# Experts' first product: both activation halves in one 512-column matmul, and every other weight subtraction on GpSimd

## The chip, the cores and the metric

The kernel runs on one core of one Trainium2 chip. The metric is device time in microseconds, the median of the timed runs. A core has five engines with an instruction queue each: PE (TensorE, matmuls, with the weight loads shown as PEld), DVE (VectorE), ACT (ScalarE), POOL (GpSimd) and SP (SyncE, which here issues the loads). Matmuls read their operands from SBUF and write to PSUM, in banks of 512 fp32 numbers per partition.

## The reference

Two transformer blocks run one after the other on 256 tokens of width 1024. The change concerns the feed-forward part of the first one, a layer of 16384 single-neuron experts:

```
q = (t @ w_peer_q) ...                       # two half queries for each of 8 heads
s1, s2 = scores of q against 128 + 128 sub-keys
v1, i1 = top_k(s1, 16); v2, i2 = top_k(s2, 16)
sc, pos = top_k(all 256 sums v1 + v2, 16)    # 16 experts for each head
gates = softmax(sc)
act = gelu(einsum('nkd,nd->nk', expert_u[e], xt), approximate=False)
return einsum('nk,nkd->nd', g * act, expert_v[e])
```

The kernel does not gather the chosen experts. It computes Gelu of the product of all 16384 rows of `expert_u` with all tokens (the first product), builds a dense matrix of gates G that is zero for experts not chosen, and multiplies the weighted activations with all of `expert_v` (the second product).

## The kernel before

Numbers are fp32, but each matrix operand is split into two numbers of a shorter format (fp32r): a high half, which is the operand rounded by a cast, and a low half, which is the operand minus the high half. A product is then the sum of three matmuls: high by high, high weights by low activations, and low weights by high activations (`mm3`, lines 226 to 228).

A unit of weights is 128 rows by 1024. `load` brings one with one DMA from SP, and `halve` splits it: a cast on ACT writes the high half (line 209), a subtraction on DVE writes the low half (line 211).

The first product takes 128 blocks of 128 experts. `up()` does one block: it issues the split of the next block's weights, keeps three loads ahead, runs `mm3` into one PSUM bank (24 matmuls of 256 columns, eight groups of three), and Gelu on ACT from PSUM into a staging tile (line 818). Every second block the tile is stored to DRAM by a DMA from ACT. The second product later reads it back.

Work of the router is woven between the blocks by `beside()`: each generator yields a cost in ns, and as many blocks are issued as that cost divided by a slack. `route` picks the top experts on DVE (slack 1300 ns, DVE's order kept as written); its last part, `keys`, compares, multiplies and reduces pieces of 256 and 512 elements (lines 676 to 680). `gates` then builds G (slack 2050 ns): for each group of eight tokens DVE makes one-hot tiles in fp16 by four instructions of 1024 elements (lines 729 to 736), PE multiplies them in 16 matmuls that `flush()` places behind a block's own (lines 744 and 745), and ACT moves the result to G (line 746). Except for DVE during `route`, the order on an engine is that of a scheduler.

Weight halves live in pools of two buffers each. While `route` runs there is a second pair of pools (`room(qs, 2)`), so four high and four low buffers; in the gates and after them there are two of each. PSUM banks for products come from `bank()`, which turns among two banks plus those that `more_banks` adds: four while `route` runs, two afterwards.

Of the kernel before, what the change touches and what calls it, by code (L numbers as in the profile page):

```python
# [8 lines left out]
F32 = mybir.dt.float32  # L9
# [10 lines left out]
T = 256  # L20
# [116 lines left out]
class Net:  # L137
# [65 lines left out]

    def halve(self, raw):
        nc = self.nc
        whi, wlo = self.turns[0]
        self.turns = self.turns[1:] + self.turns[:1]
        hi = whi.tile([128, 1024], F32R, name="hi_t", tag="hi")
        nc.scalar.copy(hi, raw)  # L209
        lo = wlo.tile([128, 1024], F32R, name="lo_t", tag="lo")  # L210
        nc.vector.tensor_tensor(lo, raw, hi[:].bitcast(F32), op=OP.subtract)  # L211
        return hi, lo
# [17 lines left out]
    def proj(self, src, x, n, s=slice(0, None), ps=None):  # L230
        ps = self.bank() if ps is None else ps
        self.mm3(ps[:, :n], self.early.pop(0) if self.early else self.unit(src), x[0], x[1], s)
        return ps[:, :n]

    def act_table(self, name):
# [526 lines left out]
    def experts(self, h, follow):  # L762
# [4 lines left out]
        with ExitStack() as es:  # L767
# [7 lines left out]
            self.slots = [pool.tile([128, T], F16, name=f"slot{i}") for i in range(4)]  # L775
            xh = pool.tile([128, KC, T], F32R, name="yh")
            xl = pool.tile([128, KC, T], F32R, name="yl")
            x = (xh, xl)
            qs = ExitStack()
            self.room(qs, 2)  # L780
            self.more_banks(qs, 2)
            qp = qs.enter_context(tc.tile_pool(name="pq", bufs=1))
# [25 lines left out]
            def up():  # L808

                nonlocal a, b, w  # L810
                nxt = self.halve(raw.pop(0)) if b + 1 < NB else None
                ahead(3)
                ps = self.bank()
                self.mm3(ps[:, :T], w, xh, xl)
                flush()
                if b % NG == 0:
                    a = stage.tile([128, NG, T], F32, name="ge_t", tag="ge")
                nc.scalar.activation(a[:, b % NG, :], ps[:, :T], AF.Gelu)
                if b % NG == NG - 1:
                    nc.scalar.dma_start(act[b // NG], a)  # L820
                w = nxt
                b += 1

            def flush():
# [29 lines left out]
            while b < NB:  # L854
                up()
            xs.close()
            self.manual = ExitStack()
# [374 lines left out]


class Acc:

# [75 lines left out]
```

## Time and profile before

| | us |
|---|---|
| median of 3 timed runs | 1465.78 (1465.11 to 1466.89) |
| the profiled execution | 1465.32, span of its instructions 1463.5 |
| first product: routing | about 192 to 405 |
| first product: gates, then a tail | about 405 to 580 |
| second product | about 580 to 960 |
| busy: PE / DVE / ACT / POOL | 1445.6 / 1089.7 / 744.6 / 0.2 |

The time of an engine is its busy time, from records whose matmul ends are modelled: a matmul record includes its latency, so the distance from one start to the next says what it costs. An idle time before an instruction is shown with the instruction that ended it. Rows of DVE and ACT that overlap by a few per cent are instructions whose record starts before that of the one ahead ends.

### The profile page before, as it was taken

What the parts mean: (1) busy time and instruction counts of PE and PEld (TensorE: products, weight loads), DVE (VectorE), ACT (ScalarE), POOL (GpSimd) and SP (SyncE); (2) the same over time, 40 slices, a digit from 0 to 9 for tenths busy, and PEclk for the clock granted to TensorE, in tenths of its full rate; (3) what the DMA queues carried; (4) which work ended last, traced back from release to release, by engine and by line L of the source; (5) the groups of instructions that cost most, each with busy time, mean ns of one, the idle gap of its engine ahead of it and who ended that gap; (6) DMA issues with size and microseconds to landing.
All of it is one profiled execution on the core that took longest, in us unless ns stands there. A gap on an engine that the chain in (4) does not pass through costs nothing.

```text
span 1463.5 us, 29428 instructions
## 1 busy us (share of the span) xinstructions
PE 1445.6 (99%) x12086; PEld 1415.1 (97%) x12086; DVE 1089.7 (74%) x1819; ACT 744.6 (51%) x1157; POOL 0.2 (0%) x4
## 2 busy tenths in 40 slices
PE   7999999999999999999999999999999999999998
PEld 7998999999999999999999999999988999999997
DVE  6975889989889997677777777797766656765554
ACT  6556554445456665544444444454455444744444
POOL 0000000000000000000000000000000000000000
PEclk9999999999999999999999999999999999999999
DMA  7333456767755556777777777745533655566662
GB/s 276 116 109 104 151 187 218 238 226 229 229 170 185 187 188 203 251 245 229 230 230 227 230 228 230 220 150 171 162 127 116 181 184 184 188 208 185 186 186 72
DMA packets 86646, 279.32 MB, mean 191 GB/s; under 512 B 9760, under 2 KB 10480, under 8 KB 86384
## 3 DMA queue, kind: packets, MB, share of 16 engines
q1 hardware_dynamic: 77296, 260.67, 56.9%
q10 hardware_dynamic: 9216, 16.78, 3.0%
q8 instruction: 94, 1.54, 0.4%
q14 instruction: 40, 0.33, 0.1%
HBM read 259.52 MB, written 17.83 MB: 189 GB/s over the span
## 4 chain that ended last, share of the span: by engine, by line
PE 94%; DVE 3%; ACT 2%; DMA 1%; issue 1%; SPq 0%; DVEq 0%; ACTq 0%
PE mm_t L226 18%; PE mm_t L228 18%; PE mm_t L227 18%; PE acc L265 10%; PE acc L266 10%; PE acc L264 10%; PE ga_t L744 1%; PE ga_t L745 1%; ACT hi_t L209 1%; DVE lo_t L211 1%; PE g_t L483 1%; DMA raw_t<-in_w 0%; PE sc_t L624 0%; PE lg_t L950 0%; PE oo_t L976 0%
## 5 line engine op out<-in xcount | busy, mean ns | idle before, releaser
L211 DVE TENSOR_TENSOR lo_t<-raw_t,hi_t 128x1024 fp32r<-128x1024 f32 x456 | 554.7, 1221 | 209.3 <-ACT hi_t L209 207.4
L209 ACT CAST hi_t<-raw_t 128x1024 fp32r<-128x1024 f32 x456 | 476.2, 1048 | 454.5 <-PE mm_t L227 312.1
L226 PE MATMUL mm_t<-yh,hi_t 128*128 128x256 f32 x1024 | 293.0, 286 | 0.0
L265 PE MATMUL acc<-vl_t,hi_t 128*128 128x256 f32 x1024 | 290.2, 283 | 0.5 <-DVE vl_t L219 0.4
L228 PE MATMUL mm_t<-yh,lo_t 128*128 128x256 f32 x1024 | 290.3, 284 | 0.1
L264 PE MATMUL acc<-vh_t,hi_t 128*128 128x256 f32 x1024 | 290.0, 283 | 0.0
L266 PE MATMUL acc<-vh_t,lo_t 128*128 128x256 f32 x1024 | 290.0, 283 | 0.0
L227 PE MATMUL mm_t<-yl,hi_t 128*128 128x256 f32 x1024 | 289.9, 283 | 0.0
L265 PEld LDWEIGHTS acc<-vl_t,hi_t 128*128 128x128 f32 x1024 | 196.7, 192 | 0.9 <-DVE vl_t L219 0.9
L228 PEld LDWEIGHTS mm_t<-yh,lo_t 128*128 128x128 f32 x1024 | 196.4, 192 | 1.1 <-DVE lo_t L211 0.8
L227 PEld LDWEIGHTS mm_t<-yl,hi_t 128*128 128x128 f32 x1024 | 196.6, 192 | 0.1
L264 PEld LDWEIGHTS acc<-vh_t,hi_t 128*128 128x128 f32 x1024 | 196.7, 192 | 0.0
L226 PEld LDWEIGHTS mm_t<-yh,hi_t 128*128 128x128 f32 x1024 | 196.4, 192 | 0.2
L266 PEld LDWEIGHTS acc<-vh_t,lo_t 128*128 128x128 f32 x1024 | 196.7, 192 | 0.0
L226 PE MATMUL mm_t<-ah,hi_t 128*128 128x256 f32 (+2 forms) x448 | 130.0, 290 | 0.0
L228 PE MATMUL mm_t<-ah,lo_t 128*128 128x256 f32 (+2 forms) x448 | 127.3, 284 | 0.0
L227 PE MATMUL mm_t<-al,hi_t 128*128 128x256 f32 (+2 forms) x448 | 126.9, 283 | 0.0
L226 PE MATMUL mm_t<-u,hi_t 128*128 128x256 f32 (+1 forms) x384 | 112.2, 294 | 7.7 <-ACT hi_t L209 7.3
L218 ACT CAST vh_t<-va_t 128x512 fp32r<-128x512 f32 x64 | 39.7, 620 | 149.2 <-DVE va_t L872 144.1
L228 PE MATMUL mm_t<-u,lo_t 128*128 128x272 f32 (+1 forms) x384 | 111.5, 291 | 0.5 <-DVE lo_t L211 0.5
L227 PE MATMUL mm_t<-u,hi_t 128*128 128x256 f32 (+1 forms) x384 | 110.6, 289 | 0.0
L227 PE MATMUL mm_t<-ol,hi_t 128*128 128x256 f32 x384 | 108.0, 281 | 0.3 <-DVE ol L219 0.3
(383 smaller groups left out, 2633.7 us busy)
## 6 DMA issues: line engine op xcount, KB each, us to landing
raw_t<-in_eu SPq DMA_DIRECT2D x128, 512.0 KB, 3.9
raw_t<-in_ev SPq DMA_DIRECT2D x128, 512.0 KB, 4.3
raw_t<-in_w2c SPq DMA_DIRECT2D x40, 512.0 KB, 3.6
act<-ge_t ACTq DMA_DIRECT2D x64, 256.0 KB, 3.3
va_t<-act SPq DMA_DIRECT2D x64, 256.0 KB, 3.3
raw_t<-in_w SPq DMA_DIRECT2D x25, 512.0 KB, 3.9
raw_t<-in_w2qkv SPq DMA_DIRECT2D x24, 512.0 KB, 3.6
raw_t<-in_wg SPq DMA_DIRECT2D x22, 512.0 KB, 4.2
```

The lines of the kernel that those rows point to most:

```text
L209: nc.scalar.copy(hi, raw)
L211: nc.vector.tensor_tensor(lo, raw, hi[:].bitcast(F32), op=OP.subtract)
L218: self.nc.scalar.copy(hi, x)
L226: nc.tensor.matmul(ps, hi[:, ks], xhi[:, k, s], start=k == 0, stop=False)
L227: nc.tensor.matmul(ps, hi[:, ks], xlo[:, k, s], start=False, stop=False)
L228: nc.tensor.matmul(ps, lo[:, ks], xhi[:, k, s], start=False, stop=k == KC - 1)
L264: mm(out, hi, a[0], start=first and opens, stop=False, skip_group_check=True)
L265: mm(out, hi, a[1], start=False, stop=False, skip_group_check=True)
L266: mm(out, lo, a[0], start=False, stop=last, skip_group_check=True)
L483: nc.tensor.matmul(ps[:, 2 * c + w, :].rearrange("p (n j) -> p n j", j=m), k, half(k, 1)[:, 0], start=c + w == 0, stop=True, skip_group_ch ...
L744: nc.tensor.matmul(out, o2[:, u, :], oh[:, :, u, :], start=i == 0, stop=False, skip_group_check=True)
L745: nc.tensor.matmul(out, o2[:, u, :], ol[:, :, u, :], start=False, stop=True, skip_group_check=True)
```

## The change

Three things change, all in the first product.

The activation halves lie in one tile `yy`, high and low half of the same 128 rows side by side. `pairs()` takes the place of `mm3`: the high weights stream both halves in one matmul of 512 columns that fills a whole bank (the first 256 columns hold high by high, the others high by low), and the low weights add their 256 columns to the first half. The last of the eight groups has the two in reverse order. A block is 16 matmuls.

The two halves of the bank are added afterwards, by `finish()`, which `up()` calls once the next block's matmuls are issued: ACT copies the second half to the staging tile, DVE adds the first half to it, and ACT applies Gelu in place. One bank more stays after `route` (three in place of two), and one fewer of the extra ones ends with it, so four remain while it runs.

The low half of every other block's weights is subtracted on POOL in place of DVE (64 of 128).

```diff
--- before.py
+++ after.py
@@ -201,14 +201,14 @@
         self.nc.sync.dma_start(raw, src)
         return raw
 
-    def halve(self, raw):
+    def halve(self, raw, vector=True):
         nc = self.nc
         whi, wlo = self.turns[0]
         self.turns = self.turns[1:] + self.turns[:1]
         hi = whi.tile([128, 1024], F32R, name="hi_t", tag="hi")
         nc.scalar.copy(hi, raw)
         lo = wlo.tile([128, 1024], F32R, name="lo_t", tag="lo")
-        nc.vector.tensor_tensor(lo, raw, hi[:].bitcast(F32), op=OP.subtract)
+        (nc.vector if vector else nc.gpsimd).tensor_tensor(lo, raw, hi[:].bitcast(F32), op=OP.subtract)
         return hi, lo
 
     def unit(self, src):
@@ -231,6 +231,19 @@
         ps = self.bank() if ps is None else ps
         self.mm3(ps[:, :n], self.early.pop(0) if self.early else self.unit(src), x[0], x[1], s)
         return ps[:, :n]
+
+    def pairs(self, w, x, s=slice(0, T)):
+
+
+        ps = self.bank()
+        pair = ps[:].rearrange("p (n t) -> p n t", n=2)
+        hi, lo = w
+        for k in range(KC):
+            ks = slice(k * 128, (k + 1) * 128)
+            parts = [(pair, hi[:, ks], x.both[:, k, :, s]), (ps[:, 0:T], lo[:, ks], x.both[:, k, 0, s])]
+            for out, a, y in parts if k < KC - 1 else reversed(parts):
+                self.nc.tensor.matmul(out, a, y, start=k == 0 and out is pair, stop=k == KC - 1 and out is pair, skip_group_check=True)
+        return ps
 
     def act_table(self, name):
         self.tc.keep_in_program_order(self.nc.scalar.preload_act_table_set(name))
@@ -773,12 +786,12 @@
             psp = xs.enter_context(tc.tile_pool(name="pep", bufs=2, space=PSUM))
             self.iota = pool.tile([128, 128], F16, name="iota16")
             self.slots = [pool.tile([128, T], F16, name=f"slot{i}") for i in range(4)]
-            xh = pool.tile([128, KC, T], F32R, name="yh")
-            xl = pool.tile([128, KC, T], F32R, name="yl")
-            x = (xh, xl)
+            x = Halves(pool, T, "yy")
+            xh, xl = x
             qs = ExitStack()
             self.room(qs, 2)
-            self.more_banks(qs, 2)
+            self.more_banks(xs)
+            self.more_banks(qs)
             qp = qs.enter_context(tc.tile_pool(name="pq", bufs=1))
             with tc.tile_pool(name="pen", bufs=2) as npool:
                 self.load_con(npool, "conp")
@@ -807,19 +820,31 @@
 
             def up():
 
-                nonlocal a, b, w
-                nxt = self.halve(raw.pop(0)) if b + 1 < NB else None
+                nonlocal b, w
+                nxt = self.halve(raw.pop(0), b % 2 == 1) if b + 1 < NB else None
                 ahead(3)
-                ps = self.bank()
-                self.mm3(ps[:, :T], w, xh, xl)
+                ps = self.pairs(w, x)
                 flush()
-                if b % NG == 0:
-                    a = stage.tile([128, NG, T], F32, name="ge_t", tag="ge")
-                nc.scalar.activation(a[:, b % NG, :], ps[:, :T], AF.Gelu)
-                if b % NG == NG - 1:
-                    nc.scalar.dma_start(act[b // NG], a)
+                finish()
+                ready.append((ps, b))
                 w = nxt
                 b += 1
+
+            ready = []
+
+            def finish():
+
+                nonlocal a
+                for ps, b in ready:
+                    if b % NG == 0:
+                        a = stage.tile([128, NG, T], F32, name="ge_t", tag="ge")
+                    y = a[:, b % NG, :]
+                    nc.scalar.copy(y, ps[:, T:2 * T])
+                    nc.vector.tensor_tensor(y, ps[:, 0:T], y, op=OP.add)
+                    nc.scalar.activation(y, y, AF.Gelu)
+                    if b % NG == NG - 1:
+                        nc.scalar.dma_start(act[b // NG], a)
+                ready.clear()
 
             def flush():
                 for f in self.after:
@@ -853,6 +878,7 @@
             vp0 = gside.enter_context(tc.tile_pool(name="vp0", bufs=1, side="right"))
             while b < NB:
                 up()
+            finish()
             xs.close()
             self.manual = ExitStack()
             self.manual.enter_context(tc.manual_schedule(engines=ordered))
@@ -1231,6 +1257,21 @@
                     nc.sync.dma_start(self.out[:, f:f + n, :], y)
 
 
+class Halves:
+
+
+    def __init__(self, pool, n, name):
+        self.both = pool.tile([128, KC, 2, n], F32R, name=name)
+
+    def __getitem__(self, i):
+        if not 0 <= i < 2:
+            raise IndexError(i)
+        return self.both[:, :, i, :]
+
+    def __len__(self):
+        return 2
+
+
 class Acc:
```

On PE, in routing, two blocks meet like this before (each row is one matmul: output, moving operand, weights; numbers tell buffers apart):

```order
L227 MATMUL mm_t_2478<-yl_1923,hi_t_2427 128x256
L228 MATMUL mm_t_2478<-yh_1922,lo_t_2429 128x256
L226 MATMUL mm_t_2478<-yh_1922,hi_t_2427 128x256
L227 MATMUL mm_t_2478<-yl_1923,hi_t_2427 128x256
L228 MATMUL mm_t_2478<-yh_1922,lo_t_2429 128x256
L226 MATMUL mm_t_2523<-yh_1922,hi_t_2472 128x256
L227 MATMUL mm_t_2523<-yl_1923,hi_t_2472 128x256
L228 MATMUL mm_t_2523<-yh_1922,lo_t_2474 128x256
```

And now:

```order
L245 MATMUL mm_t_2413<-yy_1922,hi_t_2380 128x512
L245 MATMUL mm_t_2413<-yy_1922,lo_t_2382 128x256 x2
L245 MATMUL mm_t_2413<-yy_1922,hi_t_2380 128x512
L245 MATMUL mm_t_2452<-yy_1922,hi_t_2407 128x512
L245 MATMUL mm_t_2452<-yy_1922,lo_t_2409 128x256
L245 MATMUL mm_t_2452<-yy_1922,hi_t_2407 128x512
```

A group of three has become a pair, the next block's low weights are wanted by its second matmul, and the high weights of a block are held until its last one.

On DVE, in the gates, before (`o_t`, `ol_t` and `oh_t` are the one-hot tiles, `lo_t` the low half of weights):

```order
L211 TENSOR_TENSOR lo_t<-raw_t,hi_t 128x1024
L729 TENSOR_TENSOR o_t<-iota_1917,slot_1919 128x1024
L732 TENSOR_TENSOR ol_t<-ioT,run_5713 128x1024
L735 TENSOR_TENSOR oh_t<-ol_t,run_5750 128x1024
L211 TENSOR_TENSOR lo_t<-raw_t,hi_t 128x1024
L736 TENSOR_TENSOR ol_t<-ol_t,run_5753 128x1024
L211 TENSOR_TENSOR lo_t<-raw_t,hi_t 128x1024
```

And now, where `ge_t<-mm_t,ge_t` is the add:

```order
L211 TENSOR_TENSOR lo_t<-raw_t,hi_t 128x1024
L843 TENSOR_TENSOR ge_t<-mm_t,ge_t 128x256
L742 TENSOR_TENSOR o_t<-iota_1917,slot_1919 128x1024
L745 TENSOR_TENSOR ol_t<-ioT,run_5630 128x1024
L843 TENSOR_TENSOR ge_t<-mm_t,ge_t 128x256
L748 TENSOR_TENSOR oh_t<-ol_t,run_5661 128x1024
L749 TENSOR_TENSOR ol_t<-ol_t,run_5664 128x1024
L742 TENSOR_TENSOR o_t<-iota_1917,slot_1919 128x1024
L745 TENSOR_TENSOR ol_t<-ioT,run_5630 128x1024
L211 TENSOR_TENSOR lo_t<-raw_t,hi_t 128x1024
```

Every block has an add in DVE's row, with gate work and a subtraction behind it, and every second subtraction has left the row for POOL, where the 64 stand alone.

On ACT, in the gates, the evacuation of a block before (`G` is the move of a gate group out of PSUM):

```order
L209 CAST hi_t_6988<-raw_t_6833 128x1024
L746 ACTIVATE G_5227<-ga_t_6960 128x512
L746 ACTIVATE G_5227<-ga_t_6970 128x512
L818 ACTIVATE ge_t_6924<-mm_t_6935 128x256
L820 DMA act53_1897<-ge_t_6924 128x512
L209 CAST hi_t_7032<-raw_t_6877 128x1024
```

And now, for two blocks:

```order
L842 COPY ge_t_6610<-mm_t_6523 128x256
L209 CAST hi_t_6620<-raw_t_6483 128x1024
L759 ACTIVATE G_4775<-ga_t_6590 128x512
L759 ACTIVATE G_4775<-ga_t_6600 128x512
L844 ACTIVATE ge_t_6610<-ge_t_6610 128x256
L842 COPY ge_t_6610<-mm_t_6573 128x256
L844 ACTIVATE ge_t_6610<-ge_t_6610 128x256
L846 DMA act56_1900<-ge_t_6610 128x512
L209 CAST hi_t_6658<-raw_t_6521 128x1024
```

The second block's copy stands behind a cast, two moves of G and the first block's Gelu, and its own Gelu, which waits for DVE's add, stands ahead of the next cast.

Outside the first product the order on every engine is the same as before.

## Rows read from the trace of the kernel before

**Rows 1.** Page, part 1: engine, busy us (share of the span), instructions.
```profile
PE 1445.6 (99%) x12086; PEld 1415.1 (97%) x12086; DVE 1089.7 (74%) x1819; ACT 744.6 (51%) x1157; POOL 0.2 (0%) x4
```

**Rows 2.** Windows by stage: length, busy us (count) of PE, PEld, DVE, ACT, POOL; clock.
```profile
192.00:405.00 213.00, 213.00 (x1776) 213.00 (x1777) 193.76 (x548) 103.03 (x153) 0.00 (x0) 1.00 0.70 227
424.50:567.00 142.50, 142.50 (x1415) 141.34 (x1414) 131.88 (x152) 89.20 (x175) 0.00 (x0) 1.00 0.59 186
567.00:580.00 13.00, 13.00 (x127) 12.91 (x126) 7.44 (x8) 6.86 (x13) 0.00 (x0) 1.00 0.70 221
```

**Rows 3.** Page, part 5: group, count | busy us, mean ns | idle before it.
```profile
L211 DVE TENSOR_TENSOR lo_t<-raw_t,hi_t 128x1024 fp32r<-128x1024 f32 x456 | 554.7, 1221 | 209.3 <-ACT hi_t L209 207.4
L209 ACT CAST hi_t<-raw_t 128x1024 fp32r<-128x1024 f32 x456 | 476.2, 1048 | 454.5 <-PE mm_t L227 312.1
L226 PE MATMUL mm_t<-yh,hi_t 128*128 128x256 f32 x1024 | 293.0, 286 | 0.0
```

**Rows 4.** Timeline, routing, PE: start us, us, what.
```profile
260.01 0.28 PE L226 MATMUL mm_t<-yh,hi_t 128*128 128x256 f32 x1
260.37 0.28 PE L226 MATMUL mm_t<-yh,hi_t 128*128 128x256 f32 x1
```

**Rows 5.** Windows, two periods of the gates (columns as in rows 2).
```profile
430.23:440.78 10.55, 10.55 (x106) 10.46 (x105) 10.37 (x14) 6.62 (x14) 0.00 (x0) 1.00 0.63 198
440.78:451.33 10.55, 10.55 (x106) 10.46 (x105) 9.65 (x12) 6.55 (x14) 0.00 (x0) 1.00 0.61 189
```

**Rows 6.** Timeline, gates, DVE.
```profile
503.73 1.22 DVE L211 TENSOR_TENSOR lo_t<-raw_t,hi_t 128x1024 fp32r<-128x1024 f32 x1
504.86 1.22 DVE L729 TENSOR_TENSOR o_t<-iota,slot 128x1024 f16<-128x1024 f16 x1
506.00 0.68 DVE L732 TENSOR_TENSOR ol_t<-ioT,run 128x1024 f16<-128x1024 f16 x1
506.71 0.69 DVE L735 TENSOR_TENSOR oh_t<-ol_t,run 128x1024 f16<-128x1024 f16 x1
507.32 1.22 DVE L211 TENSOR_TENSOR lo_t<-raw_t,hi_t 128x1024 fp32r<-128x1024 f32 x1
```

**Rows 7.** Timeline, gates, ACT.
```profile
502.14 1.05 ACT L209 CAST hi_t<-raw_t 128x1024 fp32r<-128x1024 f32 x1 [1.35 <-PE mm_t L227]
503.10 1.08 ACT L746 ACTIVATE G<-ga_t 128x512 f32<-128x512 f32 x2
505.98 1.05 ACT L209 CAST hi_t<-raw_t 128x1024 fp32r<-128x1024 f32 x1 [1.53 <-PE mm_t L227]
```

**Rows 8.** Waits in the gates: us in total, times, longest us.
```profile
ACT hi_t L209 <- PE mm_t L227: 51.4, 40, 1.6
```

**Rows 9.** Groups by form, gates: the comparison, once a gate group.
```profile
L729 DVE TENSOR_TENSOR o_t<-iota,slot 128x1024 f16<-128x1024 f16 x32 | 39.0, 1218 | 0.0
```

**Rows 10.** Timeline, mixer, PE: 416 columns and what follows.
```profile
63.67 0.35 PE L395 MATMUL z_t<-sp,negtri_r 128*128 128x416 f32 x1
63.85 0.29 PE L395 MATMUL z_t<-sp,negones_r 128*128 128x144 f32 x2
64.33 0.35 PE L395 MATMUL z_t<-sp,negtri_r 128*128 128x416 f32 x1
64.52 0.29 PE L395 MATMUL z_t<-sp,negones_r 128*128 128x144 f32 x2
```

**Rows 11.** Groups by form: one PSUM input on ACT and on DVE.
```profile
L818 ACT ACTIVATE ge_t<-mm_t 128x256 f32<-128x256 f32 x128 | 48.5, 379 | 3.5 <-PE mm_t L228 3.5
L1195 DVE TENSOR_TENSOR sg_t<-sg_t,mm_t 128x256 f32<-128x256 f32 x20 | 8.4, 420 | 12.1 <-PE mm_t L228 12.1
```

**Rows 12.** Groups by form: key steps of routing, DVE.
```profile
L680 DVE TENSOR_REDUCE ki<-eq 128x32 f32<-128x512 f16 x16 | 18.1, 1128 | 0.5
L678 DVE TENSOR_TENSOR eq<-eq,kf 128x256 f16<-128x256 f16 x32 | 12.1, 421 | 0.0
L676 DVE TENSOR_TENSOR eq<-io,df 128x256 f16<-128x256 f16 x32 | 7.8, 287 | 0.0
```

## The prediction

> **What bounds the kernel now.** Read the page's first part first: the reader is to see TensorE (PE) at 99% of the span and GpSimd (POOL) idle but for 0.2 us [rows 1]. Then the windows, since that share is an average: the change touches only the stage of the first product, which falls into routing (192 to 405 us), gates (424.5 to 567) and a short tail [rows 2]. In all three the TensorE clock is 1.00, its 2.4 GHz level, and PE is busy without a gap. VectorE (DVE) is the next engine: 193.8 of 213 us in routing, 131.9 of 142.5 in the gates.
>
> Then the costliest groups [rows 3]: one line of the product has 1024 matmuls, and three lines of that form make 128 blocks of 24. The 286 ns of one are latency, not price. The price is the distance of starts: three matmuls take 260.37 - 260.01 = 0.36 us, so 120 ns each and 2.88 us a block [rows 4]. Its 256 columns at 2.4 GHz are 107 ns, so 13 ns come on top.
>
> In the gates three blocks and two gate groups repeat every 10.55 us [rows 5]. Three blocks are 8.64 us, so the matmuls of a gate group cost (10.55 - 8.64) / 2 = 0.95 us. DVE works 10.37 and 9.65 us of two such periods. Its instructions there nearly all read two tensors from SBUF, and they start 1.13 us apart behind a 1.22 us subtraction or comparison and about 0.7 us behind the shorter ones [rows 6]. The cast of a high half waits for TensorE: 51.4 us in 40 waits, since there are only two high buffers there [rows 8], and it runs when a block ends (502.14, 505.98) [rows 7]. There are 32 gate groups, so 16 such periods [rows 9].
>
> **The change, part by part.**
>
> *Matmuls.* 24 of 256 columns become 8 of 512 and 8 of 256. Columns stay the same; 8 starts and 8 weight loads go. The trace has no such matmul of 512 columns. The floor by the clock is 512 / 2.4 = 213 ns; the ceiling, two of today's, is 240. The nearest row is the one of 416 columns, which is followed after 0.18 and 0.19 us [rows 10]; with 96 more columns at 120 / 256 ns, that is 225 to 235. I take 230, with 120 for the other one: 350 ns a pair in place of 360, 80 ns a block, 2.80 us a block. For all 128 blocks this is 10 us at most, unless the second one of a pair also gets cheaper: 213 + 107 = 320 would be 41 us.
>
> *Evacuation.* Before, one Gelu reads PSUM (379 ns). Now ScalarE (ACT) copies half of the bank, DVE adds the other half, and ACT runs Gelu from SBUF. I price copy and Gelu at that row's 0.38 us each, and the add at the 0.42 us of an add or product of one PSUM and one SBUF tensor of the same size [rows 11]. ACT has room (103 of 213 us in routing) [rows 2]. DVE gains 0.42 us a block and loses 1.13 / 2. What is new is the coupling: the add waits for the copy, the copy for the block's end, and behind the add stands all of DVE's routing or gate work and the next subtraction.
>
> *Half the subtractions on POOL.* No row shows a POOL instruction of this kind. From below it costs what DVE takes, 1.22 us; from above, two blocks, 5.6 us, at which POOL alone would set the pace. I take 2.44, twice the DVE row. The Trainium skill (GPSIMD Engine Reference, Performance versus the Vector engine) gives 4497 ns for 2048 elements of such an add, so by estimate 2.25 for 1024; with it the sum below would be 4.6 us lower. Whether it also stops DVE no row shows either: beside each other it costs DVE nothing, in turn it costs the whole 2.44 us. I choose in turn, the dearer end: nearly all of DVE's work in the gates has the same form as POOL's, two inputs from SBUF, and that is the stage with the least spare time. The Trainium skill (SBUF — State Buffer, Who interferes with whom) says the same: a VectorE instruction with two SBUF inputs and a GpSimd one that reads SBUF exclude each other for a whole instruction. By that rule the gates get slower, without it they stay as they are; no run here shows it yet.
>
> *Routing, 74 blocks.* TensorE saves 74 x 0.08 = 5.9 us. High buffers are four deep there, so a late POOL result is covered. DVE's work stays in its written order. In the key steps, 16 pieces of 1.13 + 2 x 0.42 + 2 x 0.29 = 2.55 us [rows 12] stand against a budget of 1700 / 1300 = 1.31 blocks: per block 2.55 / 1.31 + 0.61 + 0.42 = 2.98 us, above the 2.80 of TensorE. Before, DVE could run ahead to make that good; now the adds tie it to TensorE. 0.18 x 1.31 x 16 = 3.7 us back.
>
> *Gates, 16 periods of three blocks.* TensorE would need 10.55 - 0.24 = 10.31 us. DVE's two-input work is 2 x (1.13 + 0.7 + 0.7 + 0.7) = 6.46, plus 1.5 subtractions of 1.13 = 1.7, together 8.2; POOL's in turn 1.5 x 2.44 = 3.66. That is 11.8 us if the adds (3 x 0.42) all fall beside POOL, and 1.2 us more than before. 16 x 1.2 = 19.4 us. The order of ACT makes it no better: a copy stands behind a cast (1.05), two gate evacuations (1.08) and a Gelu, 2.9 us after the block's end, and DVE waits at the add for it. What is late next is the low half of the block after.
>
> *Tail, 6 blocks.* Two high buffers and no gate group between: a cast ends 1.2 us after a block's end, POOL 2.44 later, with a hand-over 3.75; the low half is wanted at 2.80 + 0.23 = 3.03. 0.7 late, three times: 2.1, less 0.5 of matmuls: 1.6 us.
>
> *Sum.* -5.9 + 3.7 + 19.4 + 1.6 = +18.8. The profiled run took 1465.3 us (span 1463.5), 0.5 below the median of the timed runs; 1465.3 + 18.8 = 1484. A POOL instruction of 1.94 to 2.94 us (24 of them in the gates, 12 us either way) and a matmul of 225 to 235 ns (3 us either way) give 1469 to 1499 for this case.
>
> **Rivals.**
>
> *A, beside each other:* POOL stops nobody. DVE's sum per period in the gates is then 8.2 + 1.26 = 9.5 and fits in 10.31, so the gates give 16 x 0.24 = 3.8 less. -5.9 - 3.8 + 1.6 and half the key steps, 1.9: -6.2, so 1459. For it: DVE waits 209 us before its subtractions over the whole run, so much of its row has room [rows 3]. Against it: 131.9 of 142.5 us busy in the gates.
>
> *B, cheap matmuls:* the weight load hides behind 512 columns, 216 + 120 = 336 a pair, 192 ns a block, with A's absence of stalls: 24.6 less, 1441. For it: 13 ns over the columns at 256 look like a fixed price of each matmul. Against it: at 416 columns the excess is 10 to 17 ns, no smaller.
>
> *C, cancelling:* POOL and DVE collide half the time; the gates lose 7 to 8 us, routing and tail win 4 to 6. Within 0.2% (2.9 us, about what a measurement of this kernel can tell from no change): 1466.
>
> *D, the slow side:* DVE's adds hide beside nothing, because DVE stands at an add whose copy is late while POOL could have had its turn, and then both want to go. Per period 8.2 + 1.26 + 3.66 = 13.1, 2.6 more than before, 41 us: 1506 with the other terms. It decides from the point at which the low half of every POOL block comes later than its block's first 512 columns end. For it: the copy 2.9 us behind the block's end. Against it: a DVE that waits leaves POOL undisturbed.
>
> That the change doesn't do what it says is no rival: the order shows the pairs, the adds and 64 POOL subtractions in place.
>
> **How the numbers follow.** Forecast (1484, 1469 to 1499) 0.50; A 0.19; B 0.07; C 0.09; D 0.15. Faster by over 0.2%: A and B, 0.26. Same: C, 0.09. Slower: forecast and D, 0.65. The range of 8 in 10 reaches down into A and up to D's price: 1454 to 1504; below it lie B and a part of A, above it half of D.
>
> **What would show it.** In the profile after: starts of 512 columns about 230 ns from the next, and a block of 2.80 us in routing where nothing waits; POOL near 64 x 2.44 = 156 us; in the gates a period of about 11.8 us, TensorE waiting for a low half from POOL or DVE, and DVE records there that grew while POOL is busy (in-turn shows as longer DVE instructions or as idle time before them). A period of 10.3 us with DVE records as long as before would make the forecast wrong and A right; a pair of 336 ns and idle-free gates would make B right. A routing stage of over 2.9 us a block would mean that the adds' coupling costs more than I gave it.

## The result, and the profile after

The changed kernel takes 1510.39 us (median, 1509.49 to 1511.74) against 1465.46 of the kernel before in the same rounds: 1.031 times, 95% interval 1.0294 to 1.0321. The forecast was slower, 1484 in a range of 1454 to 1504. The direction was right; the loss is 45 us where 18.8 were forecast, and the time lies above the range.

Where the 45 us are is read from the starts of the blocks' first matmuls in the two traces. Routing is cut in two here: top-k (blocks 1 to 48) and key steps (48 to 76); the gates are blocks 76 to 122, 15.33 periods of three blocks; the tail is the last six, up to the first matmul of the second product (at 591.6 us before, not at about 580).

| us from first matmul to first matmul | before | after | difference | forecast |
|---|---|---|---|---|
| top-k, 47 blocks | 135.4 | 135.9 | +0.5 | -3.8 |
| key steps, 28 blocks | 81.5 | 93.7 | +12.2 | +1.5 |
| gates, 46 blocks | 162.8 | 192.3 | +29.5 | +19.4 |
| tail, 6 blocks | 18.6 | 21.6 | +3.0 | +1.6 |

What follows the tail takes 872 us in both, and what comes ahead of block 1 is 1.3 us shorter after. The page's first part after, as in [rows 1]: PE fell from 99% to 96%, POOL went from nothing to 169 us.

```profile
PE 1452.9 (96%) x11062; PEld 1358.9 (90%) x11062; DVE 1137.9 (75%) x1883; ACT 787.3 (52%) x1285; POOL 168.9 (11%) x68
```

The windows of top-k, key steps and gates, first before and then after; columns as in [rows 2]:

```profile
193.40:328.80 135.40, 135.40 (x1131) 135.40 (x1130) 123.97 (x413) 65.36 (x97) 0.00 (x0) 1.00 0.70 228
328.80:410.20 81.40, 81.40 (x680) 81.28 (x679) 71.13 (x130) 37.80 (x57) 0.00 (x0) 1.00 0.71 227
410.20:573.00 162.80, 162.38 (x1602) 160.89 (x1601) 150.46 (x174) 100.91 (x201) 0.00 (x0) 1.00 0.58 182
```

```profile
192.10:328.00 135.90, 133.84 (x754) 114.87 (x753) 125.13 (x446) 79.59 (x141) 57.20 (x23) 1.00 0.66 216
328.00:421.60 93.60, 81.53 (x455) 68.34 (x454) 85.04 (x149) 49.09 (x87) 35.17 (x14) 1.00 0.62 202
421.60:613.90 192.30, 171.10 (x1233) 141.43 (x1231) 183.42 (x196) 115.33 (x246) 63.65 (x22) 0.98 0.48 155
```

The reader is to see DVE, the third busy time, in the last row of each: 150.46 of 162.8 us before, 183.4 of 192.3 after. PE has room there (171.1, its matmul latencies included), where before it had next to none. The clock in that row is 0.98 because TensorE ran at 1.2 GHz in two stretches, 497.6 to 501.0 and 548.8 to 552.2 us, after stretches in which PE had waited (busy 4.8 of 6.6 us and 5.2 of 6.8). A pair took 0.64 us there in place of 0.35, so by estimate the two cost 3 us at most; no term of the forecast had them. The first of the two:

```profile
497.60:501.00 3.40, 3.40 (x13) 2.92 (x11) 3.30 (x3) 0.88 (x5) 2.46 (x1) 0.50 0.52 154
```

The matmuls did what they were to do. Two groups of PE's timeline in top-k, as in [rows 4]:

```profile
251.09 0.28 PE L245 MATMUL mm_t<-yy,lo_t 128*128 128x256 f32 x1
251.21 0.40 PE L245 MATMUL mm_t<-yy,hi_t 128*128 128x512 f32 x1
251.46 0.28 PE L245 MATMUL mm_t<-yy,lo_t 128*128 128x256 f32 x1
251.57 0.40 PE L245 MATMUL mm_t<-yy,hi_t 128*128 128x512 f32 x1
```

A group takes 0.37 us here between the first and third row and 0.36 between the second and fourth; over all of them the median is 234 ns behind 512 columns and 117 behind 256, 351 ns against 350 forecast. The subtractions in the costliest groups, as in [rows 3]:

```profile
L211 DVE TENSOR_TENSOR lo_t<-raw_t,hi_t 128x1024 fp32r<-128x1024 f32 x392 | 492.2, 1259 | 181.2 <-ACT hi_t L209 180.1
L211 POOL TENSOR_TENSOR lo_t<-raw_t,hi_t 128x1024 fp32r<-128x1024 f32 x64 | 168.7, 2637 | 463.6 <-ACT hi_t L209 460.3
```

The median of one on POOL is 2.41 us (2.44 forecast); the mean of 2.64 holds its waits for DVE. Eight microseconds of DVE's row in the gates, as in [rows 6], and POOL's beside it:

```profile
505.98 1.22 DVE L742 TENSOR_TENSOR o_t<-iota,slot 128x1024 f16<-128x1024 f16 x1
507.12 2.87 DVE L749 TENSOR_TENSOR ol_t<-ol_t,run 128x1024 f16<-128x1024 f16 x1
509.91 0.41 DVE L843 TENSOR_TENSOR ge_t<-mm_t,ge_t 128x256 f32<-128x256 f32 x1
510.25 0.68 DVE L745 TENSOR_TENSOR ol_t<-ioT,run 128x1024 f16<-128x1024 f16 x1
510.96 0.69 DVE L748 TENSOR_TENSOR oh_t<-ol_t,run 128x1024 f16<-128x1024 f16 x1
511.68 0.69 DVE L749 TENSOR_TENSOR ol_t<-ol_t,run 128x1024 f16<-128x1024 f16 x1
512.32 1.23 DVE L211 TENSOR_TENSOR lo_t<-raw_t,hi_t 128x1024 fp32r<-128x1024 f32 x1
513.46 0.42 DVE L843 TENSOR_TENSOR ge_t<-mm_t,ge_t 128x256 f32<-128x256 f32 x1
```

```profile
506.17 3.27 POOL L211 TENSOR_TENSOR lo_t<-raw_t,hi_t 128x1024 fp32r<-128x1024 f32 x1 [6.11 <-ACT hi_t L209]
```

POOL starts at 506.17 while DVE's line 742 runs until 507.2, and ends at 509.44. DVE's line 749 starts at 507.12 and takes 2.87 us where it takes 0.69 four rows further down. So first POOL waited for DVE, then DVE for POOL: the two were in turn. The add (line 843) starts only when that is over, at 509.91, beside nothing.

Split by whether POOL's subtraction was running when a DVE instruction started, the medians of all records of the first product are, clear against beside: line 745 0.68 against 2.88 us (7 of 32), line 748 0.68 against 2.53 (13), the comparison of line 689 0.28 against 1.74 (4), DVE's own subtraction 1.22 against 1.79 (16). Those with at most one input from SBUF stay as they are: the add, which reads PSUM and SBUF, 0.414 against 0.413 us (31 of 128), MAX8 0.28 in both. The Trainium skill (SBUF — State Buffer, Who interferes with whom) states this rule; the trace agrees, for the two-input form and for the one-input form.

### The profile page after: what moved, and what is told of

Read it like the earlier page. It is cut to its first block, busy times and chain, and to the rows that moved or that the text cites. A ratio compares the mean times of both kernels' runs of the same rounds, so it can differ in the third digit from the quotient of the medians.

```text
span 1507.7 us, 27726 instructions
## 1 busy us (share of the span) xinstructions
PE 1452.9 (96%) x11062; PEld 1358.9 (90%) x11062; DVE 1137.9 (75%) x1883; ACT 787.3 (52%) x1285; POOL 168.9 (11%) x68
## 4 chain that ended last, share of the span: by engine, by line
PE 68%; DVE 13%; issue 11%; POOL 5%; ACT 2%; DMA 0%; POOLq 0%; SPq 0%; DVEq 0%; ACTq 0%
PE acc L278 10%; PE acc L279 10%; PE acc L277 10%; PE mm_t L226 10%; PE mm_t L228 10%; PE mm_t L227 10%; POOL lo_t L211 5%; DVE lo_t L211 4%; PE mm_t L245 2%; DVE ge_t L843 1%; DVE eq L691 1%; DVE rest_t L618 1%; DVE eq L689 1%; ACT hi_t L209 1%; DVE ki L693 1%
## 5 line engine op out<-in xcount | busy, mean ns | idle before, releaser
L211 DVE TENSOR_TENSOR lo_t<-raw_t,hi_t 128x1024 fp32r<-128x1024 f32 x392 | 492.2, 1259 | 181.2 <-ACT hi_t L209 180.1
L245 PE MATMUL mm_t<-yy,hi_t 128*128 128x512 f32 x1024 | 364.3, 402 | 7.5 <-ACT hi_t L209 7.5
L245 PE MATMUL mm_t<-yy,lo_t 128*128 128x256 f32 x1024 | 272.8, 287 | 29.3 <-DVE lo_t L211 24.5
L245 PEld LDWEIGHTS mm_t<-yy,lo_t 128*128 128x128 f32 x1024 | 194.8, 190 | 53.1 <-DVE lo_t L211 36.6
L245 PEld LDWEIGHTS mm_t<-yy,hi_t 128*128 128x128 f32 x1024 | 187.9, 190 | 42.7 <-ACT hi_t L209 10.3
L211 POOL TENSOR_TENSOR lo_t<-raw_t,hi_t 128x1024 fp32r<-128x1024 f32 x64 | 168.7, 2637 | 463.6 <-ACT hi_t L209 460.3
L844 ACT ACTIVATE ge_t<-ge_t 128x256 f32<-128x256 f32 x128 | 53.3, 419 | 106.5 <-DVE ge_t L843 106.1
```

The costliest lines, as they stand in the source:

```text
L211: (nc.vector if vector else nc.gpsimd).tensor_tensor(lo, raw, hi[:].bitcast(F32), op=OP.subtract)
L245: self.nc.tensor.matmul(out, a, y, start=k == 0 and out is pair, stop=k == KC - 1 and out is pair, skip_group_check=True)
L844: nc.scalar.activation(y, y, AF.Gelu)
```

## The experiments

Times are medians; ratios are to the kernel before, run in the same rounds. The stages are those of the table above, from the profiled execution. The code cuts show only the lines that differ; "..." stands for lines left out.

| run | us | ratio, 95% | top-k | keys | gates | tail |
|---|---|---|---|---|---|---|
| before | 1465.5 | | 135.4 | 81.5 | 162.8 | 18.6 |
| after | 1510.4 | 1.031 (1.0294 to 1.0321) | 135.9 | 93.7 | 192.3 | 21.6 |
| e1 pairs, DVE only | 1480.0 | 1.0105 (1.0088 to 1.0122) | 140.3 | 90.5 | 161.6 | 18.8 |
| e2 POOL only | 1501.9 | 1.0252 (1.0235 to 1.0269) | 135.4 | 87.4 | 192.5 | 19.8 |
| e3 halves of 256 | 1489.5 | 1.0167 (1.0151 to 1.0184) | 146.4 | 92.1 | 163.2 | 18.6 |
| e4 POOL in top-k | 1477.1 | 1.0082 (1.0065 to 1.0098) | 135.9 | 91.9 | 161.6 | 18.9 |
| e5 split each | 1484.0 | 1.0126 (1.011 to 1.0141) | 135.4 | 81.8 | 180.0 | 19.2 |
| e7 bystander | 1512.1 | 1.0322 (1.0297 to 1.0347) | 135.4 | 99.6 | 187.9 | 20.0 |
| e8 late finish | 1474.1 | 1.0062 (1.0046 to 1.0077) | 132.5 | 87.6 | 161.5 | 19.1 |
| e9 hybrid | 1468.0 | 1.0017 (1.0008 to 1.0026) | 136.0 | 82.1 | 161.6 | 20.0 |
| e10 copy bystander | 1474.3 | 1.0066 (1.0049 to 1.0082) | 135.4 | 83.7 | 169.4 | 18.8 |
| e11 low last | 1505.9 | 1.0277 (1.0262 to 1.0293) | 133.3 | 91.8 | 192.2 | 19.7 |
| e12 POOL, low last | 1500.8 | 1.0242 (1.0227 to 1.0258) | 135.4 | 88.4 | 190.6 | 19.5 |
| e13 hybrid, late | 1469.1 | 1.0023 (1.0014 to 1.0032) | 139.7 | 82.2 | 164.8 | 19.2 |
| e14 no adds in gates | 1497.9 | 1.0228 (1.0211 to 1.0245) | 135.9 | 93.7 | 181.8 | 19.7 |
| e15 quarter in gates | 1494.2 | 1.0202 (1.0185 to 1.0219) | 135.9 | 93.8 | 174.5 | 21.5 |

### The parts by themselves: e1, e2, e3, e4

e1, the changed kernel with all subtractions on DVE:

```diff
-nxt = self.halve(raw.pop(0), b % 2 == 1) if b + 1 < NB else None
+nxt = self.halve(raw.pop(0)) if b + 1 < NB else None
```

> The change without its POOL part: pairs, copy, add and Gelu stay, all 128 subtractions on DVE. In-turn theory (POOL's subtraction and DVE's two-input instructions exclude each other, that is most of the 45 us): DVE has 0.57 us a block more to do, but nothing blocks it. Routing's top-k part 1.47 + 1.13 + 0.42 = 3.02 us a block in place of 2.88, +6; key steps 1.95 + 1.13 + 0.42 = 3.5, +10; gates 8.2 + 1.7 + 1.26 = 11.2 us a period in place of 10.55, +10. About 1490, faster than the change. Coupling theory (DVE waits in its order for ACT's copies, POOL is harmless and relieves DVE): 1510 or more, since DVE has more to do.

The gates are whole again, 161.6 us, where 10 us more than before were expected. So without POOL that stage loses nothing. Top-k (+4.9) and key steps (+9.0) lose by pairs alone. Its windows:

```profile
193.00:333.30 140.30, 134.73 (x754) 114.19 (x753) 136.96 (x469) 81.90 (x141) 0.00 (x0) 1.00 0.66 215
333.30:423.70 90.40, 82.48 (x455) 67.99 (x454) 85.01 (x165) 50.71 (x87) 0.00 (x0) 1.00 0.67 210
423.70:585.30 161.60, 160.94 (x1234) 137.86 (x1232) 160.23 (x217) 116.25 (x246) 0.00 (x0) 1.00 0.57 185
```

DVE is busy 160.2 of 161.6 us in the gates, 99%. Before it had 12.3 us to spare there; the adds have used that up, and little is left to take in what POOL costs DVE.

e2, the kernel before with every other subtraction on POOL:

```diff
-nc.vector.tensor_tensor(lo, raw, hi[:].bitcast(F32), op=OP.subtract)
+(nc.vector if vector else nc.gpsimd).tensor_tensor(lo, raw, hi[:].bitcast(F32), op=OP.subtract)
 ...
-nxt = self.halve(raw.pop(0)) if b + 1 < NB else None
+nxt = self.halve(raw.pop(0), b % 2 == 1) if b + 1 < NB else None
```

> The kernel before with the POOL part alone: every other subtraction on POOL, matmuls and Gelu as before. In-turn theory: DVE instructions with two SBUF inputs that start during a POOL subtraction last until its end, as in the changed kernel; gates 8.2 + 3.66 = 11.9 us a period, +21; key steps +8; top-k part nothing: 1494. Coupling theory: there is no add and no copy, DVE is relieved by 0.57 us a block: 1465, no change.

POOL alone costs 2.5%, 8 us more than expected: 29.7 us in the gates, 5.9 in the key steps, nothing in top-k, whose MAX8 and FIND_INDEX8 read one tensor. In its window of the gates DVE is idle for 20.7 us, not 8.9 as after, and the clock is 0.96:

```profile
415.70:608.10 192.40, 172.78 (x1601) 167.51 (x1601) 171.75 (x152) 100.21 (x201) 64.81 (x22) 0.96 0.47 154
```

e3, e1 with the 512-column matmul as two of 256 into the two halves of the bank:

```diff
-parts = [(pair, hi[:, ks], x.both[:, k, :, s]), (ps[:, 0:T], lo[:, ks], x.both[:, k, 0, s])]
+parts = [(ps[:, 0:T], hi[:, ks], x.both[:, k, 0, s]), (ps[:, T:2 * T], hi[:, ks], x.both[:, k, 1, s]), (ps[:, 0:T], lo[:, ks], x.both[:, k, 0, s])]
```

> As the run with pairs and all subtractions on DVE, but the pair is taken apart again: 24 matmuls of 256 columns, high by low into the second half of the bank. What differs is the 512-column matmul alone. If DVE sets the pace in most of the stage: the same time as that run, within 3 us. If TensorE does: 128 blocks x 0.06 us = 8 us more.

Against e1 it is 9.5 us slower: that is the worth of the wide matmuls, near the 10 us worked out before. By stage the agreement is partly luck: 6.1 us lie in top-k, where 80 ns a block would give 3.8, and 1.6 in the gates, where they would give 3.7. Against the kernel before it is 24 us slower: the price of copy, add and second pass of ACT, with the banks as they are after. The gain did not cover it.

e4, the changed kernel with POOL for the first 48 blocks only:

```diff
-nxt = self.halve(raw.pop(0), b % 2 == 1) if b + 1 < NB else None
+nxt = self.halve(raw.pop(0), b % 2 == 1 or b >= 48) if b + 1 < NB else None
```

> The change with POOL subtracting only in the first 48 blocks, beside the top-k search, whose instructions read one SBUF tensor; from block 48 on DVE subtracts. In-turn theory: blocks up to 48 at 2.82 us as in the changed kernel, key steps and gates as in the run without POOL (+10 and +10), 1484, the fastest of the runs with pairs. Coupling theory: 1505 or more, as DVE has more to do where it has least room.

1477.1, 7 us below what was expected: of the 45 us, 33 go away with POOL out of key steps, gates and tail. In top-k POOL gives back 4.4 of the 4.9 us that pairs cost there.

### In turn, or late? e5, e7, e11, e12

In the gates the loss could be POOL's hold on DVE (in turn), or its result arriving late for the next block (two high buffers). e7 puts POOL work beside the kernel before that nobody waits for but the raw tile's next load:

```diff
 nc.vector.tensor_tensor(lo, raw, hi[:].bitcast(F32), op=OP.subtract)
+if extra:
+    nc.gpsimd.tensor_tensor(raw, raw, raw, op=OP.add)
 ...
-nxt = self.halve(raw.pop(0)) if b + 1 < NB else None
+nxt = self.halve(raw.pop(0), b % 2 == 0) if b + 1 < NB else None
```

> The kernel before with all subtractions on VectorE; behind every other one GpSimd also adds the used raw tile to itself in place (two inputs, 128x1024 fp32). Nobody waits for that but the raw tile's next load. In-turn theory: VectorE's 9.75 us per three blocks in the gates plus 1.5 x 2.4 = 3.7 us give 13.4 in place of 10.55, 16 times: +45 us; the key steps lose 6 to 20 us, the top-k stage (one input from SBUF) nothing: 1510 to 1530, and VectorE's two-input instructions that start beside GpSimd are 1 to 2 us longer. Rival, lateness of GpSimd's result: nobody waits for it here, so 1465, with VectorE's instructions as long as before.

+47 us, with no result of POOL's in use: lateness is not needed for such a loss. The gates lose 25 us, where 45 were expected: DVE's instructions there are stretched by about 37 us in all (their length beyond the median of those clear of POOL), and 10 us of that came out of DVE's idle time (12.3 us before, 2.1 now). The key steps lose 18. DVE's row in the gates, with POOL's instruction at 465.24:

```profile
465.03 1.22 DVE L731 TENSOR_TENSOR o_t<-iota,slot 128x1024 f16<-128x1024 f16 x1
466.16 2.38 DVE L734 TENSOR_TENSOR ol_t<-ioT,run 128x1024 f16<-128x1024 f16 x1
468.58 0.69 DVE L737 TENSOR_TENSOR oh_t<-ol_t,run 128x1024 f16<-128x1024 f16 x1
```

```profile
465.24 2.75 POOL L213 TENSOR_TENSOR raw_t<-raw_t 128x1024 f32<-128x1024 f32 x1 [6.15 <-DVE lo_t L211]
```

e5, the kernel before with each low half made in two pieces, DVE 512 columns and POOL the other 512, which are wanted half a block later:

```diff
+for e, s in ((nc.vector, slice(0, 512)), (nc.gpsimd, slice(512, 1024))):
+    e.tensor_tensor(lo[:, s], raw[:, s], hi[:, s].bitcast(F32), op=OP.subtract)
```

> The kernel before (256-column matmuls, Gelu from PSUM), but every block's low half is made in two pieces: VectorE subtracts the first 512 columns, GpSimd the last 512. GpSimd has the same columns in all as with every other whole block, but its result comes half as late and is wanted later (the matmuls of the last four slices). In-turn theory (a GpSimd subtraction and a VectorE instruction with two inputs from SBUF exclude each other): the time that GpSimd takes from VectorE in the gates is the same 1.5 x 2.4 us per three blocks, so the gates lose 25 to 32 us again: 1490 to 1500. Rival, lateness (GpSimd's result comes late for the two high buffers of the gates, and VectorE loses nothing by itself): the pieces come in time, gates as before, 1463 to 1470.

Between the two: the gates lose 17 us, not 30. The stretch of DVE's instructions there is 32 to 35 us in place of 45 after, so a smaller loss fits in turn as well; by itself this run settled nothing.

e11, the changed kernel with a block's low-half matmuls behind seven of its eight wide ones:

```diff
-for k in range(KC):
+steps = [("h", k) for k in range(KC - 1)] + [("l", k) for k in range(KC)] + [("h", KC - 1)]
+for which, k in steps:
 ...
```

> The changed kernel with a block's matmuls in another order: seven of the eight 512-column ones, then the eight on the low half, then the last 512-column one, so that the low half is wanted some 1.4 us later in the block (7 x 0.234 us in place of 0.23) and the high half is released no sooner. Work, engines and buffers are the same. Lateness theory (what the gates lose is that GpSimd's result, started only when a high buffer comes free and stretched by the exclusion, comes after the block it belongs to has begun): most of the 29.5 us of the gates comes back, 164 to 175 us there in place of 192, 1480 to 1493 in all. Rival, load theory (the exclusion takes so much of VectorE's time that VectorE sets the period): gates stay at 188 to 193 us, 1505 to 1511.

The gates did not move, 192.2 us, with DVE as busy as in the changed kernel:

```profile
418.10:610.30 192.20, 167.94 (x1233) 142.33 (x1231) 183.60 (x196) 115.51 (x246) 62.15 (x22) 0.98 0.49 156
```

e12, the same order in e2:

```diff
-self.mm3(ps[:, :T], w, xh, xl)
+self.mm3_low_late(ps[:, :T], w, xh, xl)
 ...
+steps = [("h", k) for k in range(KC - 1)] + [("l", k) for k in range(KC)] + [("h", KC - 1)]
```

> The run with GpSimd's subtractions alone in the kernel before (1501.9 us, gates 192.5), with the eight matmuls on the low half moved behind fourteen of the sixteen on the high half (low half wanted 1.7 us into the block in place of 0.24). No adds here. Lateness theory: gates 163 to 172 us, 1470 to 1481. Load theory: gates stay at 188 to 193, 1497 to 1502. If this one recovers and the changed kernel with the low half last does not, the adds hold VectorE there.

190.6 us against 192.5. A low half wanted 1.4 to 1.7 us later buys at most 2 us: its lateness is not what the gates lose by. PE still waits in e11, but now for the high half (18.7 us in 16 waits), with DVE's load unchanged. Lateness is there in the tail, where e11 has 19.7 us against 21.6.

### What the adds cost in the gates: e14, and the dose: e15

e14, the changed kernel with no copy and no add from block 76. It leaves the product of high weights and low activations out of those blocks' result, though PE still works it out:

```diff
+if b < 76:
     nc.scalar.copy(y, ps[:, T:2 * T])
     nc.vector.tensor_tensor(y, ps[:, 0:T], y, op=OP.add)
-nc.scalar.activation(y, y, AF.Gelu)
+nc.scalar.activation(y, y if b < 76 else ps[:, 0:T], AF.Gelu)
```

> The changed kernel, but from block 76 on ScalarE's Gelu reads the first half of the bank straight, with no copy and no add: the high weights' product with the low half of the activations is left out of those blocks' result (its columns are still streamed). Same GpSimd subtractions. Theory that the adds lie exposed in VectorE's row in the gates (each starts the next instruction 0.33 us later, 45 of them: 15 us): gates 175 to 181 us in place of 192, 1492 to 1497. Rival, the adds fill time in which VectorE would have waited anyway (the run with GpSimd alone, without adds, takes as long in the gates): 188 to 193 us, 1506 to 1511.

e15, the changed kernel with every fourth subtraction on POOL from block 76:

```diff
-nxt = self.halve(raw.pop(0), b % 2 == 1) if b + 1 < NB else None
+nxt = self.halve(raw.pop(0), b % (2 if b < 76 else 4) != 0) if b + 1 < NB else None
```

> The changed kernel with every fourth instead of every second subtraction on GpSimd from block 76 on. By the run with none there (161.6 us) and the changed kernel (192.3) the exclusion as a price of each GpSimd instruction gives half of the difference: gates 175 to 179 us, 1493 to 1497 in all. Rival, a chain that only every-second-block use sets up (GpSimd's result late for the block behind it): VectorE has the free block to catch up, gates 162 to 168, 1480 to 1486.

The gates of e14, then of e15:

```profile
421.90:603.70 181.80, 166.24 (x1234) 140.14 (x1233) 173.58 (x153) 100.80 (x202) 60.68 (x22) 0.98 0.53 165
```

```profile
421.90:596.40 174.50, 163.50 (x1234) 138.07 (x1232) 173.08 (x208) 114.22 (x244) 30.99 (x11) 1.00 0.55 170
```

Without copies and adds the gates are 10.5 us shorter, though not the 11 to 17 expected: 181.8 / 15.33 = 11.86 us a period. e15, just below the 175 to 179 us expected of it, with 11 POOL subtractions there, loses 12.9 us to e1 and the changed kernel, with 22, loses 30.7: 1.2 and 1.4 us each, on top of the 1.14 us of the DVE subtraction that each one spares. That makes 2.3 and 2.5 us, close to the 2.41 of a subtraction on POOL. The price goes with the number of POOL instructions, and DVE is busy 173.1 of 174.5 us.

### One input on GpSimd: e10

e7 with a copy in place of the sum:

```diff
-    nc.gpsimd.tensor_tensor(raw, raw, raw, op=OP.add)
+    nc.gpsimd.tensor_copy(raw, raw)
```

> As the bystander run (kernel before, a GpSimd instruction behind every second subtraction that nobody waits for; 1512.1 us), but a copy of the raw tile onto itself, one input from SBUF in place of two. If any reading of SBUF by GpSimd holds back VectorE's two-input instructions, the loss is in proportion to GpSimd's busy time, 20 to 47 us: 1485 to 1512, with records of VectorE that are longer by a GpSimd copy. If only two-input instructions of both engines exclude each other: 1463 to 1468, VectorE's records as long as before.

It cost 9 us, less than expected, because the copy takes 1.04 us when nothing stops it and POOL's time beyond that is waiting. But it excludes too: line 734 of DVE takes 1.53 us in place of 0.68 beside a POOL copy that started at 466.92.

```profile
463.54 0.68 DVE L734 TENSOR_TENSOR ol_t<-ioT,run 128x1024 f16<-128x1024 f16 x1
...
467.86 1.53 DVE L734 TENSOR_TENSOR ol_t<-ioT,run 128x1024 f16<-128x1024 f16 x1
```

### Key steps, and a better version: e8, e9, e13

e8, e4 with the evacuation one block later still:

```diff
-finish()
+finish(1)
```

> The run with GpSimd in the top-k stage alone (first 48 blocks; 1477.1 us, key steps 91.9 us in place of 81.5), with the evacuation of a block put off by one block more, so that ScalarE's copy of its half of the bank is long done when VectorE comes to the add. Theory that the key steps lose by the coupling (VectorE stands at the add waiting for the copy, the copy waits for the block's end): key steps back to 80 to 84 us, 1466 to 1469. Rival, load (VectorE's own 0.42 us a block more is what the key steps lack): key steps stay at 90 to 93 us, 1475 to 1479.

87.6 us in the key steps, between the two theories, with the profiled execution 4 us below the median of the timed ones. As far as this one execution shows, 4 of the 10 us are coupling and the rest is load: DVE is busy 83.8 of 87.6 us there, 85 in e1 and 71.1 before. In top-k every block took 2.82 us, and PE waited for nothing.

e9 uses pairs and POOL in top-k, the form of before in the key steps, and pairs without POOL from block 76:

```diff
+nxt = self.halve(raw.pop(0), b % 2 == 1 or b >= 46) if b + 1 < NB else None
+two = b < 46 or b >= 76
+if two:
+    ps = self.pairs(w, x)
+else:
+    ps = self.bank()
+    self.mm3(ps[:, :T], w, xh, xl)
 ...
```

> Pairs with every other subtraction on GpSimd for the first 46 blocks (top-k stage); the kernel before's 256-column matmuls and subtractions on VectorE, with no add, for blocks 46 to 75 (key steps); pairs with all subtractions on VectorE from block 76 (gates, tail). Theory that each stage is charged by itself: top-k +0.5, key steps 0, gates -1.2 us: 1463 to 1466, the same as before within 0.2%. Rival: the stages before are coupled (VectorE carries a debt from the top-k stage into the key steps, since the adds hold it to TensorE's pace there): key steps lose 3 to 8 us, 1468 to 1474.

Top-k, key steps and gates are each charged by themselves, within 1 us of what was expected of them; the whole, 1468.0, lies 2 us above the expected range and is no faster than the kernel before: the interval lies just above 1. e13 is e9 with e8's later evacuation:

```diff
-finish()
+finish(1)
```

> The hybrid (pairs with GpSimd for blocks 0 to 45, the kernel before's form for 46 to 75, pairs without GpSimd from 76; 1468.0 us) with the evacuation of a pair put off by one block more, which took the top-k stage from 135.9 to 132.5 us in the run with GpSimd in the top-k stage alone. By that the top-k stage gives 132.5, key steps 82, gates 161.5, tail 19: 1462 to 1465, at or 0.1 to 0.2% below the kernel before. Rival: the 3.4 us in the top-k stage were borrowed from the key steps (VectorE's later work), which then take 84 to 86: 1466 to 1469.

No gain either: its median is 1.1 us above e9's. Its profiled execution is the slowest of its eleven, 4 us above the median, so its 139.7 us in top-k are no fair measure. Four of the 47 blocks of that stage lost 7.1 us against e8's pace, and ahead of each DVE's subtraction ran into POOL's and was stretched, so that its low half came late; behind the last of them the clock stood at 1.2 GHz from 292.1 to 295.5 us. Two of the four:

```profile
280.85 3.09 DVE L211 TENSOR_TENSOR lo_t<-raw_t,hi_t 128x1024 fp32r<-128x1024 f32 x1
288.27 3.30 DVE L211 TENSOR_TENSOR lo_t<-raw_t,hi_t 128x1024 fp32r<-128x1024 f32 x1
```

```profile
280.46 2.39 POOL L211 TENSOR_TENSOR lo_t<-raw_t,hi_t 128x1024 fp32r<-128x1024 f32 x1 [1.86 <-ACT hi_t L209]
288.10 2.39 POOL L211 TENSOR_TENSOR lo_t<-raw_t,hi_t 128x1024 fp32r<-128x1024 f32 x1 [5.25 <-ACT hi_t L209]
```

Whether such meetings are why the later evacuation gains nothing in the median, no run shows. No version beats the kernel before.

## Why the prediction was wrong in size

*Matmuls:* right, 351 ns a group against 350, and 9.5 us in all (e3 against e1) against 10. In the stages that sum did not hold (e3). Rival B, the cheap matmul of 336 ns, did not come.

*POOL's price, and in turn:* right in the gates. 2.41 us against 2.44, and exclusive with DVE's two-input instructions, shown by their lengths after, by e7, and by the dose in e15. Rival A (beside each other) is refuted.

*The gates:* here is the step that failed: "if the adds (3 x 0.42) all fall beside POOL". Of the adds' 18.6 us in the gates, 3.6 lay beside a POOL instruction. The row at 505 to 513 us shows why: DVE stands in a two-input instruction while POOL works, and starts the add, next in its row, when that is over. e14 measures the step: without the adds and their copies, which it does not tell apart, a period is 11.86 us, the forecast's 11.8; with them it is 192.3 / 15.33 = 12.54. That is 0.7 us times 15.33, 10.5 us, and it accounts for the gates' difference from the forecast (29.5 against 19.4). The clock is not behind it: 6.8 us of the gates ran at 1.2 GHz in e14 as after. It is rival D at a little over half its price, and not by D's way: D put three adds at 1.26 us, and they cost 0.7; one takes 0.33 us from start to start, and no add in the gates waited for its copy.

That e14 meets 11.8 is in part luck. The forecast had 8.2 us of DVE's work and 3.66 of POOL's in turn, and no idle time; e14 has about 8.3 of work, 3.0 of stretch (about 46 us over the stage) and 0.5 of idle time. The forecast's "1.2 us more" is a slip besides: 8.2 + 3.66 - 10.55 is 1.3, and 16 times that is 21, not 19.4.

*The key steps:* forecast +1.5, measured +12.2. The step "0.18 x 1.31 x 16 = 3.7" left out two things. In turn was charged in the gates alone, though the comparisons and products there (lines 689 and 691) also read two tensors from SBUF:

```profile
343.96 2.63 DVE L691 TENSOR_TENSOR eq<-eq,kf 128x256 f16<-128x256 f16 x1
```

```profile
343.88 2.44 POOL L211 TENSOR_TENSOR lo_t<-raw_t,hi_t 128x1024 fp32r<-128x1024 f32 x1 [4.97 <-ACT hi_t L209]
```

Clear of POOL that line takes 0.42 us. In the trace after, the stretch of DVE's instructions in this stage is 15 to 16 us beside 14 POOL subtractions, and 14 subtractions moved away save 14 x 1.14 = 16: moving them gave nothing (e4, with all of them back on DVE, has 91.9 us against 93.7). And the pairs with their adds, without POOL, cost 9.0 (e1), part load and part coupling (e8). The prediction had named the sign: routing took (135.9 + 93.7) / 75 = 3.06 us a block, above 2.9, and six times an add waited for its copy in the key steps, 6.0 us in all.

*Top-k:* forecast -3.8, measured +0.5. The 80 ns a block were there: 41 of the 47 blocks took 2.82 us, and e8 had 2.82 in all of them, 132.5 us. The other six lost 3.4 us, because PE waited at their start for a low half that DVE, not POOL, made late. The longest four of these waits, in the list of waits of the stage:

```profile
PE mm_t L245 <- DVE lo_t L211: 2.1, 4, 0.9
```

The forecast tied DVE to PE's pace by the adds in the key steps alone; here the same tie cost what the matmuls gained. With the evacuation one block later (e8, in the execution profiled) no block waited. Without POOL, pairs lose 4.9 us (e1), and there DVE's load sets the pace: busy 137.0 of 140.3 us. Nor is POOL free beside pairs: 12 of DVE's 23 subtractions in the stage ran into POOL's and were stretched, 11.5 us in all, where in e2 none was.

*Tail:* +3.0 against 1.6; right in kind, and e11 takes 1.9 of it back.

By stage, forecast against result: 10.1 us of the miss lie in the gates, 10.7 in the key steps, 4.3 in top-k and 1.4 in the tail, 26.5 together.

Open: why e2 without adds takes as long in the gates as the changed kernel, where e14, without adds too, is 10.7 us shorter. DVE waits 12 us more in e2; it has one PSUM bank fewer, and PE waits there for a Gelu to free one, but no run tried that bank alone. TensorE also ran at 1.2 GHz for 13.6 us of e2's gates, against 6.8 in e14; by estimate, from 0.64 us a group of three there against 0.36, that is worth about 3 of the 10.7 us.

## What to carry to other kernels

Before work goes to GpSimd, count the inputs from SBUF of what VectorE does in that stage: beside instructions with two of them, GpSimd's time was taken from VectorE here, so 1.22 us moved at a price of 2.41 was a loss where VectorE had little room. An instruction is not hidden because it could run beside another: it must come up in its engine's row at that moment, so price it as exposed unless the trace shows the pairing. And a saving on the busiest engine is worth only what the next engine leaves of it, here 9.5 us of matmuls against 24 us of evacuation.

## What the hardware showed that was not expected

The exclusion needs only one input on GpSimd's side, which the expectation of e10 had left open: a plain copy, 1.04 us when nothing stops it, lengthened a two-input instruction of VectorE by 0.85 us.

VectorE can keep GpSimd out for many instructions. In e7 a POOL instruction started at 440.06 (the row below joins it, 9.8 us long, with the next), and for 8 us VectorE's two-input instructions followed each other 0.60 or 1.13 us apart, each starting before the record of the one ahead had ended. POOL came in only behind the instruction of 447.45, where the next one started 0.70 us later: 448.15, which took 2.81 us. That the short gap let POOL in is read off this place; no run tried it.

```profile
446.32 1.21 DVE L731 TENSOR_TENSOR o_t<-iota,slot 128x1024 f16<-128x1024 f16 x1
447.45 0.68 DVE L734 TENSOR_TENSOR ol_t<-ioT,run 128x1024 f16<-128x1024 f16 x1
448.15 2.81 DVE L211 TENSOR_TENSOR lo_t<-raw_t,hi_t 128x1024 fp32r<-128x1024 f32 x1
```

```profile
440.06 12.66 POOL L213 TENSOR_TENSOR raw_t<-raw_t 128x1024 f32<-128x1024 f32 x2 [10.26 <-DVE lo_t L211]
```
